# Second layer's modulation vectors: from the two second MLP products into the first layer's first MLP product and the second layer's mixers

## Chip, cores and metric

One core of a Trainium2 chip runs one inference step of a two-layer backbone. The metric is the device time of one execution in microseconds (us). Engines are named as in the profile: PE is TensorE (matmul), DVE is VectorE, ACT is ScalarE, POOL is GpSimd, SP issues the DMAs. A row of the profile names a line of the kernel (L286), the engine, the operation, and the tiles as "written<-read".

## The reference

Each of the two layers first turns a conditioning vector into six modulation vectors per conditioning row (there are two rows: the latent request and the context):

```python
m = silu(cond) @ w_mod + b_mod            # 6 * 1024 values per layer and row
sh1, sc1, g1, sh2, sc2, g2 = split(m, 6)
h  = rms_norm(x, norm1) * (1 + sc1) + sh1
mix = concat(A(h), B(h), C(h)) @ w_out    # RG-LRU, HGRN2, neighbourhood attention
x  = x + g1 * mix
h2 = rms_norm(x, norm2) * (1 + sc2) + sh2
x  = x + g2 * (square(relu(h2 @ w1)) @ w2)
```

x holds 1152 tokens (1024 latent, 128 context) of 1024 features; w1 is 1024 x 4096 and w2 is 4096 x 1024. The modulation of a layer is 48 tiles of 128 output features: tiles 0 to 7 are sh1, 8 to 15 sc1, 16 to 23 g1, 24 to 31 sh2, 32 to 39 sc2 and 40 to 47 g2. So tiles 0 to 15 are needed before a layer's first normalisation, 16 to 23 when its output projection is added to x, 24 to 39 before its MLP, and 40 to 47 only at the very end of the layer.

## The kernel before

Activations lie feature-major (128 features on the partitions, tokens along the free axis). Every large product is done in three passes over a high and a low part of each operand: ACT rounds the high part (`acopy`, L186), POOL or DVE subtracts it (`psub` L189, `vsub` L192). A layer has four stages, each written as a Python loop that a scheduler (`tc`) then orders for each engine by a simulated timeline and priorities; every engine runs its list in that order and waits where an operand is late.

1. Projections and mixers. `project` (tile `pj`) and `project_tokens` (tile `pt`) make the ten column groups; `rglru` (products `gr`, `gi`, line L740) runs beside the first of them and `hgrns` (products `sc`, L536, merged by the DVE at L541) beside the rest. `weave` alternates them in the source.
2. Attention (products `sl`, `tl`, `tc`, `av`) together with the output projection (tile `wo`), with the projections that are left over.
3. First MLP product (weights `ws`, L1110 to L1112): a one-level Strassen scheme, 16 column pairs times two token halves, 32 steps of 84 matmuls. The results are squared on ACT and DVE, combined and written to DRAM (`od`, `oraw`). Buffers `od_` (2) and `hx_` (3) are slices of one tile `spare`: in the first layer the tile that held silu(cond), named `sil`, in the second a tile `pad`.
4. Second MLP product (weights `wt`, operands `R`): 8 groups of operands come back from DRAM (`prepared_operands`), steps of 42 matmuls are accumulated in tiles `row` by the DVE (L198), the last group with the gate g2 (L210, `row<-z,mod,row`). Operands `R` take 18 slots in turn.

A modulation tile is made by `mod_tile` (L276): it loads 128 rows of the transposed w_mod into `wm` and lets the DVE multiply them by silu(cond) and sum along the row, once per conditioning row (L286, tile `junk` or `jk`); each such instruction is followed by a short one that reads its accumulator out. The tile is cut in as many pieces as the buffer is wide: with a ring of 384 columns (`g_`, or `sqt`, the four buffers of squares) three pieces, six instructions; with the ring `hr_` (1152 columns) one piece of 1024, two instructions.

Where the tiles are made, before: the first layer's 16 to 47 beside its own mixers, in small pieces (`mods`, 10 tiles beside `rglru`, 22 beside `hgrns`); the second layer's 0 to 39 in steps 2 to 44 of the first layer's second MLP product, in pieces of 1024 (`MODS2`); the second layer's 40 to 47 in the same steps of the second layer's second MLP product.

## Time and profile before

| | us |
|---|---|
| median of 3 runs | 3270.18 (3263.32 to 3278.54) |
| profiled execution | 3276.47 |
| its span, first to last instruction | 3274.7 |
| PE busy | 2960.4 (90% of the span) |
| DVE busy | 2406.1 (73%) |
| ACT busy | 1641.4 (50%) |
| POOL busy | 1567.8 (48%) |

The profiled execution lies 1.77 us above its own span and 6.3 us above the median of the runs. Busy times are shares of the whole span and mix stages with different limits; a window row gives, for one stretch, its length and then for PE, weight loads, DVE, ACT and POOL the busy time with the number of instructions in brackets, then the granted TensorE clock as a share of full speed, the busy share of the DMA engines and GB/s. The stages lie as follows: first layer's mixers to 537 us, attention and output projection to 833, first MLP product to 1235, second to 1678; second layer's mixers to 2117, attention and output projection to 2441, first MLP product to 2839, second to 3247.

### The profile page before, as it was taken

The page shows a single profiled execution, that of the slowest core. Times are in us where ns is not written, and L with a number is a line of the kernel's source. Part 1 is how long each engine was busy: PE and PEld are TensorE (multiplying, and loading weights), DVE is VectorE, ACT ScalarE, POOL GpSimd, SP SyncE. Part 2 cuts the span into 40 slices and gives each one's busy share as a digit, 9 for nine tenths or more (in the row PEclk, how much of TensorE's full clock was granted, in tenths as well). Part 3 has the DMA queues.
Part 4 walks back from the last instruction along what each step waited for, and adds up shares of the span by engine and source line. Part 5 has one row for each costly group of instructions (what it writes and reads, how often), then busy time and mean ns, then how long its engine had stood idle before and what let it go on. Part 6 is the DMA issues. An engine that isn't in the chain of part 4 may idle for free. (4 is left out here: it accounts for less than half of the span.)

```text
span 3274.7 us, 61327 instructions
## 1 busy us (share of the span) xinstructions
PE 2960.4 (90%) x21208; PEld 2815.3 (86%) x21208; DVE 2406.1 (73%) x5283; ACT 1641.4 (50%) x4079; POOL 1567.8 (48%) x1528
## 2 busy tenths in 40 slices
PE   7888998998889998988868999999987999899995
PEld 7878888798789998888858889988977999899994
DVE  8899974667885568998874677346779755777787
ACT  5543234565566666344454533345646566654443
POOL 4541132345676665554545311334556765654453
PEclk8989999999899998999979999999998999999997
DMA  7342447983455567675522102689634655855552
GB/s 270 91 108 87 132 121 224 283 269 103 158 176 185 177 212 279 216 245 198 181 94 74 58 29 80 183 239 293 220 127 148 194 179 181 281 204 173 185 194 68
DMA packets 391318, 566.48 MB, mean 173 GB/s; under 512 B 45920, under 2 KB 250848, under 8 KB 391008
## 3 DMA queue, kind: packets, MB, share of 16 engines
q1 hardware_dynamic: 391008, 562.57, 53.8%
q8 instruction: 167, 2.74, 0.4%
q14 instruction: 143, 1.17, 0.1%
HBM read 397.01 MB, written 165.42 MB: 172 GB/s over the span
## 5 line engine op out<-in xcount | busy, mean ns | idle before, releaser
L189 POOL TENSOR_TENSOR wl<-wr,wh 128x512 fp32r<-128x512 f32 x164 | 231.1, 1413 | 485.4 <-ACT wh L186 379.2
L189 POOL TENSOR_TENSOR wt<-wl,wt 128x256 fp32r<-128x256 f32 x276 | 258.0, 942 | 176.5 <-ACT wt L186 116.5
L1110 PE MATMUL bB<-R,wt 128*128 128x288 f32 x768 | 236.9, 309 | 63.7 <-ACT bB L186 40.8
L189 POOL TENSOR_TENSOR ws<-wl,ws 128x512 fp32r<-128x512 f32 x160 | 227.5, 1426 | 121.4 <-ACT ws L186 121.3
L421 PE MATMUL pj<-hh,wh 128*128 128x384 f32 x640 | 223.7, 354 | 27.0 <-ACT g L213 12.3
L1110 PE MATMUL bB<-t,ws 128*128 128x288 f32 x768 | 231.7, 302 | 18.0 <-DVE hr L198 9.6
L423 PE MATMUL pj<-hh,wl 128*128 128x384 f32 x640 | 225.1, 352 | 7.1 <-POOL wl L189 7.1
L1111 PE MATMUL bB<-R,wt 128*128 128x288 f32 x768 | 231.1, 301 | 0.0
L1112 PE MATMUL bB<-R,wt 128*128 128x288 f32 x768 | 230.0, 300 | 0.0
L1111 PE MATMUL bB<-t,ws 128*128 128x288 f32 x768 | 229.6, 299 | 0.0
L1112 PE MATMUL bB<-t,ws 128*128 128x288 f32 x768 | 229.2, 299 | 0.0
L422 PE MATMUL pj<-hh,wh 128*128 128x384 f32 x640 | 223.4, 350 | 0.0
L1110 PEld LDWEIGHTS bB<-R,wt 128*128 128x128 f32 x768 | 148.2, 193 | 74.2 <-ACT bB L186 48.3
L186 ACT CAST wt<-wl 128x256 fp32r<-128x256 f32 x288 | 115.9, 406 | 159.8 <-PE bB L1112 82.0
L421 PE MATMUL wo<-u,wh 128*128 128x288 f32 x512 | 160.1, 314 | 17.1 <-DVE x L210 13.4
L1110 PEld LDWEIGHTS bB<-t,ws 128*128 128x128 f32 x768 | 147.6, 192 | 22.0 <-DVE hr L198 11.4
L186 ACT CAST wh<-wr 128x512 fp32r<-128x512 f32 x164 | 101.1, 618 | 129.3 <-PE pj L422 65.2
L207 POOL TENSOR_SCALAR pl<-pl,rc 128x384 f32<-128x384 f32 x128 | 79.1, 618 | 176.5 <-DVE rc L952 83.9
L1110 PE MATMUL bA<-R,wt 128*128 128x288 f32 x512 | 156.0, 305 | 8.1 <-DVE row L210 5.8
L1112 PE MATMUL bA<-t,ws 128*128 128x288 f32 x512 | 155.4, 304 | 8.0 <-DVE ws L192 6.5
L1110 PE MATMUL bA<-t,ws 128*128 128x288 f32 x512 | 155.1, 303 | 4.3 <-ACT ws L186 2.3
L1111 PE MATMUL bA<-R,wt 128*128 128x288 f32 x512 | 154.6, 302 | 0.0
(363 smaller groups left out, 11364.9 us busy)
## 6 DMA issues: line engine op xcount, KB each, us to landing
wr<-in_w SPq DMA_DIRECT2D x304, 256.0 KB, 3.3
R<-od SPq DMA_DIRECT2D x96, 576.0 KB, 5.6
xb<-or SPq DMA_DIRECT2D x128, 288.0 KB, 4.2
wm<-in_w_mod SPq DMA_DIRECT2D x64, 512.0 KB, 5.6
od<-sil SPq DMA_DIRECT2D x96, 288.0 KB, 2.9
od<-pad SPq DMA_DIRECT2D x96, 288.0 KB, 3.1
wr<-in_w_in SPq DMA_DIRECT2D x104, 256.0 KB, 3.0
bi<-in_bias SPq DMA_DIRECT2D x96, 192.0 KB, 4.5
```

Of the source, the lines that this page charges most:

```text
L186: nc.scalar.copy(out=out, in_=in_)
L189: nc.gpsimd.tensor_tensor(out=out, in0=a, in1=b, op=ALU.subtract)
L207: nc.gpsimd.tensor_scalar(out=out, in0=a, scalar1=s1, scalar2=s2, op0=op0, op1=op1)
L421: mm(ps, lhsT=wh(k), rhs=ah(k), start=k == first, stop=False)
L422: mm(ps, lhsT=wh(k), rhs=al(k), start=False, stop=False)
L423: mm(ps, lhsT=wl(k), rhs=ah(k), start=False, stop=k == last)
L1110: mm(ps, lhsT=w[:, 0, ti(i)], rhs=t[:, 0], start=start and i == 0, stop=False, skip_group_check=True)
L1111: mm(ps, lhsT=w[:, 0, ti(i)], rhs=t[:, 1], start=False, stop=False, skip_group_check=True)
L1112: mm(ps, lhsT=w[:, 1, ti(i)], rhs=t[:, 0], start=False, stop=i == n - 1, skip_group_check=True)
```

## The change

- The second layer's tiles 0 to 15 are made in the first layer's first MLP product, from step 10 to step 30 of 32, through `sqt` (three pieces a tile). Since silu(cond) is needed there, it is loaded again at step 8 into the tile `sil`, which until then serves as `spare`; from then on the first layer's `od_` buffers come from `xr_` (two, as before) and `hx_` from `sqt`, the four buffers that the pieces of w_mod also use.
- Tiles 16 to 47 of the second layer are made beside its own mixers, by the same call and at the same places as in the first layer; `mods` no longer stops at the first layer. silu(cond) is kept until the second layer's mixers end, and no longer loaded in the second layer's MLP.
- Both second MLP products lose their modulation tiles, and with them the scratch tile `jk`.
- The 18 operand slots of the second MLP product are now three pools (4, 11 and 3) instead of two (7 and 11) with the turn started at the fourth slot. `gel` of the second layer comes from `g_` instead of a pool of its own, the gate weights `gw` from `xt`.

```diff
-MODS2 = (2, 44)
+MLP_MODS = (10, 30)
...
         def mods(n, piece):
             for j in take(left, n):
-                mod_tile(0, j, piece)
+                mod_tile(l, j, piece)
                 yield
 
-        left = iter(range(16, 48 if l == 0 else 16))
+        left = iter(range(16, 48))
...
+        later = iter(range(16))
         n = 0
         for v, (j, qs) in enumerate(first):
...
+                if not last and n == MLP_MODS[0] - 2:
+
+                    od_, hx_ = repeat(lambda: xr_("od")), repeat(lambda: sqt("hx")[:, :BLK])
+                    for c in range(2):
+                        load_cond(c)
+                if not last:
+                    for e in take(later, steps(16, MLP_MODS, n - 1)):
+                        mod_tile(l + 1, e, sqt)
         line.end()
...
-        tp0 = phase(st0, "tp0", 7, T, "right")
+        tp0, tp1 = phase(st0, "tp0", 4, T, "right"), phase(st0, "tp1", 3, T, "right")
...
-        junk1 = phase(st0, "jk", 1, DM // 2, "right")("jk").bitcast(mybir.dt.bfloat16)
-        tp1 = phase(st1, "tp1", 11, T, "right")
-
-        turn = cycle([tp0] * 7 + [tp1] * 11)
-        run_out(take(turn, 3))
+        tp2 = phase(st1, "tp2", 11, T, "right")
+
+        turn = cycle([tp0] * 4 + [tp2] * 11 + [tp1] * 3)
...
-        for c in range(2):
-            load_cond(c)
-        later = iter([(1, j) for j in (range(40, 48) if last else range(40))])
-        n_later, n = (8 if last else 40), 0
...
-                    n += 1
-                    for a in take(later, steps(n_later, MODS2, n)):
-                        mod_tile(*a, hr_, junk1)
```

What the engines are given can be read from the two programs' instruction lists. First the DVE in the first layer's first MLP product, one step before (`hr` and the slices of `sil` hold squared results, `wl` the sums of weights, `s` and `bB`, `bC` the product's accumulators):

```order
L198 TENSOR_TENSOR sil<-bC,s_12525 128x288
L210 SCALAR_TENSOR_TENSOR sil<-sil 128x288
L192 TENSOR_TENSOR hr<-sil,hr 128x288
L192 TENSOR_TENSOR sil<-hr,sil 128x288
L192 TENSOR_TENSOR wl<-wr 128x512
L192 TENSOR_TENSOR hr<-hr 128x288
L192 TENSOR_TENSOR sil<-sil,hr 128x288
L198 TENSOR_TENSOR hr<-bB,s_12656 128x288
L198 TENSOR_TENSOR sil<-bC,s_12656 128x288
L192 TENSOR_TENSOR wl<-wr,wl 128x512
```

and the same stretch of a step now, the slices of `sil` having become `hx`:

```order
L198 TENSOR_TENSOR hx<-bC,s_12151 128x288
L210 SCALAR_TENSOR_TENSOR hx<-hx 128x288
L192 TENSOR_TENSOR wl<-wr,wl 128x512
L192 TENSOR_TENSOR hr<-hx,hr 128x288
L192 TENSOR_TENSOR hx<-hr,hx 128x288
L192 TENSOR_TENSOR hr<-hr 128x288
L198 TENSOR_TENSOR wl<-wr 128x512
L286 ISA junk,ma<-wm,sil,par_106 128x384
L286 ISA ma 128x1
L192 TENSOR_TENSOR hx<-hx,hr 128x288
```

Between the step's own instructions stand the pieces of a modulation tile, each with its read of the accumulator; such a step has six pieces, 16 of the steps have them.

Next the DVE in the second layer's HGRN2, at the start of a block (`q`, `qb`, `kb`, `kf` are the decayed queries and keys, `ff` and `tot` the decays, `L` and `K` what the products `sc` read). Before:

```order
L198 TENSOR_TENSOR qb<-q,ff 128x384
L198 TENSOR_TENSOR q<-q,ff 128x384
L198 TENSOR_TENSOR qb<-qb,ff 128x192
L183 COPY L<-q 128x192
L183 COPY K<-kf 128x192
L198 TENSOR_TENSOR tot<-ff 128x192 x2
L198 TENSOR_TENSOR kb<-kb,ff 128x192
L198 TENSOR_TENSOR q<-q,ff 128x192
L198 TENSOR_TENSOR kf<-kf,ff 128x192
```

and now:

```order
L198 TENSOR_TENSOR qb<-q,ff 128x384
L286 ISA junk,mod_117<-wm,sil,ma 128x256
L286 ISA mod_117 128x1
L198 TENSOR_TENSOR q<-q,ff 128x384
L286 ISA junk,ma<-wm,sil,par_106 128x384
L286 ISA ma 128x1
L198 TENSOR_TENSOR qb<-qb,ff 128x192
L183 COPY L<-q 128x192
L183 COPY K<-kf 128x192
L198 TENSOR_TENSOR tot<-ff 128x192 x2
```

The same chain is now broken by pieces. From the first `xc` to the first merged `sc` there are 77 pieces among 124 other instructions, and from there to the last merged `sc` 115 among 461; the first layer has 77 among 123 and 115 among 462 there, before and now.

Last, PE at the third job of the second layer's attention (`tl` and `tc` transpose its softmax, `av` is its product with the values, `pj` are projections that are left over, `wo` is the output projection). Before, leftover projections stand between the transposes:

```order
L992 MATMUL av<-ptc,vc 64x128
L908 MATMUL sx<-ck,QS 128x256 x2
L992 MATMUL av<-ptc,vc 64x128 x3
L914 MATMUL sl<-KS,QS 128x384 x4
L967 MATMUL tl<-ident,pl 128x128 x3
L421 MATMUL pj<-hh_20201,wh 128x384
L422 MATMUL pj<-hh_20201,wh 128x384
L423 MATMUL pj<-hh_20201,wl 128x384
```

and now:

```order
L423 MATMUL pj<-hm_20376,wl 128x384
L421 MATMUL pj<-hm_20382,wh 128x384
L422 MATMUL pj<-hm_20382,wh 128x384
L423 MATMUL pj<-hm_20382,wl 128x384
L914 MATMUL sl<-KS,QS 128x384 x2
L967 MATMUL tl<-ident,pl 128x128 x6
L974 MATMUL tc<-ident,pc 128x128 x4
L421 MATMUL wo<-u,wh 128x288
L992 MATMUL av<-ptl,V 64x128 x6
L992 MATMUL av<-ptc,vc 64x128
```

In the new list the transposes of that job follow its scores with no projection between, and the output projection begins right behind them. The first layer's list has this order before and now: more of the projections stand beside HGRN2, and fewer are left for the attention.

## Rows read from the trace of the kernel before

**Rows 1.** The page: span, and part 1 (engine busy us, share, instructions).

```profile
span 3274.7 us, 61327 instructions
PE 2960.4 (90%) x21208; PEld 2815.3 (86%) x21208; DVE 2406.1 (73%) x5283; ACT 1641.4 (50%) x4079; POOL 1567.8 (48%) x1528
```

**Rows 2.** Windows, both second MLP products: stretch: length, busy (count) per engine, clock, DMA.

```profile
1247.20:1595.40 348.20, 317.43 (x2256) 310.61 (x2256) 316.73 (x612) 156.21 (x393) 179.57 (x164) 0.97 0.67 227
2851.20:3165.80 314.60, 306.07 (x2256) 303.53 (x2255) 230.61 (x467) 156.85 (x393) 152.37 (x164) 0.99 0.58 198
```

**Rows 3.** Tile row, first layer: count, ns min/median/max, first and last start, forms.

```profile
L186 ACT COPY row<-bA x8: 390/396/449, 1247.2 to 1287.8; 128x288 f32<-128x288 f32 x8
L210 DVE SCALAR_TENSOR_TENSOR row<-z,mod,row x32: 269/439/929, 1595.4 to 1671.6; 128x224 f32<-128x224 f32 x16, 128x64 f32<-128x64 f32 x16
```

**Rows 4.** Groups by form, DVE, line 286: count, busy us, mean ns.

```profile
L286 DVE CUSTOM_DVE_ANT_0 jk<-wm,sil,par 128x1024 bf16<-128x1024 f32 x96 | 136.7, 1424 | 7.8 <-ACT sil L213 4.4 <-DMA wm<-in_w_mod 3.3
L286 DVE CUSTOM_DVE_ANT_0 junk<-wm,sil,ma 128x384 bf16<-128x384 f32 x64 | 47.2, 738 | 3.6 <-DMA wm<-in_w_mod 2.8
L286 DVE CUSTOM_DVE_ANT_0 junk<-wm,sil,par 128x384 bf16<-128x384 f32 x64 | 44.7, 699 | 7.4 <-DMA wm<-in_w_mod 6.7
L286 DVE CUSTOM_DVE_ANT_0 junk<-wm,sil,ma 128x256 bf16<-128x256 f32 x64 | 38.8, 606 | 0.7
L286 DVE DVE_READ_ACCUMULATOR2_ANT mod<- 128x1 f32 x160 | 12.6, 78 | 0.0
L286 DVE DVE_READ_ACCUMULATOR2_ANT ma<- 128x1 f32 x128 | 10.3, 81 | 0.0
```

**Rows 5.** Tile wm, first layer's mixers.

```profile
L286 DVE CUSTOM_DVE_ANT_0 junk<-wm,sil,ma x128: 453/605/1669, 119.5 to 416.1; 128x384 bf16<-128x384 f32 x64, 128x256 bf16<-128x256 f32 x64
L286 DVE CUSTOM_DVE_ANT_0 junk<-wm,sil,par x64: 587/614/1694, 114.3 to 413.0; 128x384 bf16<-128x384 f32 x64
```

**Rows 6.** Waits of PE, both second MLP products: total us, times, longest.

```profile
PE bB L1110 <- ACT bB L186: 24.3, 17, 2.4
PE bB L1110 <- ACT bB L186: 6.6, 5, 2.2
```

**Rows 7.** Windows, first gr product to last wo product, both layers.

```profile
117.30:833.40 716.10, 650.32 (x4782) 592.89 (x4783) 549.21 (x1554) 317.90 (x845) 251.00 (x294) 0.95 0.54 159
1758.60:2440.70 682.10, 643.61 (x4784) 586.64 (x4783) 420.34 (x1159) 320.83 (x847) 246.85 (x294) 0.97 0.48 144
```

**Rows 8.** Windows, RG-LRU and HGRN2 stretches, both layers.

```profile
117.30:233.90 116.60, 91.40 (x491) 82.64 (x491) 103.65 (x222) 55.55 (x100) 53.76 (x46) 0.91 0.35 85
233.90:480.80 246.90, 231.24 (x1794) 211.66 (x1794) 231.62 (x731) 82.51 (x207) 55.20 (x57) 0.98 0.38 111
1758.60:1858.90 100.30, 85.19 (x464) 77.19 (x462) 49.99 (x83) 56.36 (x101) 50.25 (x46) 0.93 0.14 34
1858.90:2059.40 200.50, 195.79 (x1607) 178.09 (x1607) 155.84 (x474) 70.76 (x177) 36.19 (x39) 0.97 0.20 58
```

**Rows 9.** Waits of PE, first layer, RG-LRU to output projection.

```profile
PE pj L421 <- ACT g L213: 12.3, 1, 12.3
PE tc L974 <- ACT pc L213: 7.5, 1, 7.5
```

**Rows 10.** ACT in order of time, first attention: start us, us, group, idle before.

```profile
563.96 0.72 ACT L213 ACTIVATE ck<-ckr,sel 128x512 fp32r<-128x512 f32 x1 [8.92 <-DMA ckr<-in_cache_k]
```

**Rows 11.** Windows, second layer's projections with TensorE full.

```profile
1725.00:1750.00 25.00, 25.00 (x147) 25.00 (x146) 10.05 (x13) 9.66 (x18) 16.65 (x13) 1.00 0.40 131
```

**Rows 12.** Windows, first layer's first MLP product.

```profile
975.00:1175.00 200.00, 200.00 (x1510) 200.00 (x1509) 113.11 (x166) 121.63 (x281) 129.93 (x114) 1.00 0.57 184
1175.00:1200.00 25.00, 25.00 (x191) 25.00 (x190) 22.08 (x28) 15.74 (x36) 17.39 (x15) 1.00 0.53 169
```

**Rows 13.** Instruction groups by form, DVE, in the same stretch.

```profile
L192 DVE TENSOR_TENSOR hr<-sil,hr 128x288 f32<-128x288 f32 x21 | 20.0, 952 | 0.7
L192 DVE TENSOR_TENSOR hr<-hr 128x288 f32<-128x288 f32 x20 | 10.0, 501 | 1.1
```

More of the change, by code (lines that the diff above doesn't have):

```diff
@@ L1 @@
 from contextlib import ExitStack, nullcontext
-from itertools import cycle
+from itertools import cycle, repeat
 import concourse.bass as bass
@@ L274, in build, with mod_tile @@
     am = [C.tile([P, 16, 2], F32, name=f"am{l}") for l in range(DEPTH)]
-    def mod_tile(l, j, piece, junk=junk):
+    def mod_tile(l, j, piece):
         acc = [pcol(l, "bm", j)] * 2
@@ L1331, in e @@
             def e(n, ps):
-                gel[i][n] = (gl_ if l and n < 2 else xt)("gel")
+                gel[i][n] = (g_ if l and n < 2 else xt)("gel")
                 act(gel[i][n], ps, AF.Gelu_apprx_tanh)
@@ L1434, in build @@
                         run_out(project(win(m), ht, e, (n,)))
-        gw = [g_("gw")[:, :2 * P] for _ in range(4)]
+        gw = [(xt if l else g_)("gw")[:, :2 * P] for _ in range(4)]
         for j in range(4):
@@ L1536, in build @@
         if l:
-            gl_st.close()
+            sil_st.close()
         h_st, x4_st = ExitStack(), ExitStack()
@@ L1639, in build @@
         oraw = tc.dram_tile([NG, 2, len(SUMS), P, 2 * BLK], F32, name=f"or{l}")
-        od_ = cycle([spare[:, i * 2 * BLK:(i + 1) * 2 * BLK] for i in range(2)])
-        hx_ = cycle([spare[:, i * BLK:(i + 1) * BLK] for i in range(4, 7)])
+        od_ = cycle([lambda i=i: spare[:, i * 2 * BLK:(i + 1) * 2 * BLK] for i in range(2)])
+        hx_ = cycle([lambda i=i: spare[:, i * BLK:(i + 1) * BLK] for i in range(4, 7)])
         st = ExitStack()
@@ L1684, in part @@
             def part(p, t):
-                o = next(od_).bitcast(F32R).rearrange("p (j m) -> p j m", j=2)
+                o = next(od_)().bitcast(F32R).rearrange("p (j m) -> p j m", j=2)
                 acopy(o[:, 0], t)
@@ L1715, in c1 @@
             def c1(r, ps):
-                t = next(hx_) if r else ft("hr")[:, :BLK]
+                t = next(hx_)() if r else ft("hr")[:, :BLK]
                 act(t, ps, AF.Relu)
@@ L1721, in c2 @@
             def c2(r, ps):
-                t = ft("hr")[:, :BLK] if r else next(hx_)
+                t = ft("hr")[:, :BLK] if r else next(hx_)()
                 vtt(t, ps, on.s5, ALU.add)
@@ L1759, in build @@
             sil_st.close()
-        sil_st = ExitStack()
-        sil = phase(sil_st, "sil2", 1, 2 * DM)("sil").rearrange("p (c d) -> p c d", c=2)
+        if not last:
+            sil_st = ExitStack()
+            sil = phase(sil_st, "sil2", 1, 2 * DM)("sil").rearrange("p (c d) -> p c d", c=2)
+            for c in range(2):
+                load_cond(c)
         h_st, row_st, st0, st1 = (ExitStack() for _ in range(4))
@@ L1859, in build @@
                         st1.close()
-                        sil_st.close()
                         if not last:
-                            gl_st = ExitStack()
-                            gl_ = phase(gl_st, "gl", 4)
                             H = h_st.enter_context(tc.tile_pool(name="h", bufs=1, reuse_waits="tile"))
```

## The prediction

> **What bounds the kernel now.** I read the page first, then windows stage by stage. PE is busy for 90% of the span [rows 1], so a microsecond counts only where PE stands still or runs at half clock. The kernel holds its own comparison: each stage runs twice, once per layer, with the same matmuls and with different numbers of modulation tiles beside them.
>
> In the second MLP product, the stretch from the first copied block to the first gated add of the last group [rows 3] has 2256 matmuls in both layers. With 40 tiles (first layer) it lasts 348.2 us and DVE is busy for 316.7; with 8 tiles it lasts 314.6 with DVE at 230.6 [rows 2]. The waits say why: PE waits for ACT's copy into `bB`, which itself waits for the DVE's adds into `row`, 24.3 us in the first layer and 6.6 in the second [rows 6]. There the DVE is the bound.
>
> In the mixers, attention and output projection it is the other way round: the first layer has 32 tiles and needs 716.1 us, the second none and needs 682.1, for 4782 and 4784 matmuls [rows 7]. The excess lies in PE's idle time (65.8 against 38.5 us) and in a lower granted clock (0.95 against 0.97). In the first MLP product PE is full, at full clock, with DVE at 57% [rows 12].
>
> So the change takes tiles from a stage where they cost time, and puts two thirds of them where the first layer shows that they cost time too.
>
> **The change, part by part.** A tile in one piece is two instructions of 1.424 us and two reads of 0.078: 3.0 us of DVE. A tile in three pieces costs, from the first layer's 32, (47.2 + 44.7 + 38.8 + 10.3 + 64 x 0.078) / 32 = 4.56 us [rows 4]. The 48 moved tiles thus grow from 144 to 219 us of DVE work; by stage: -120, +73, +146, -24.
>
> (a) First layer's second MLP product loses 40 tiles. Thirty-two of them are worth 348.2 - 314.6 = 33.6 us, 1.05 us a tile. The last 8 can be worth at most what PE still idles beside them, 314.6 - 306.1 = 8.5 us [rows 2]; at least nothing. I take 4, the middle, since not all of the 6.6 us of waits [rows 6] stand near a tile. Together -37.6. The bounds: -42.1, and -17.7 if only the difference of the `bB` waits returns. What is late next is the operands `R`, as in the second layer, which the row of 314.6 contains.
>
> (b) Second layer's second MLP product loses the same 8: -4, between 0 and -8.5.
>
> (c) Second layer's mixers gain 32 tiles. The lists give them the first layer's places (77 pieces up to the first merged `sc`, 115 from there), and PE gets the first layer's order there, with few projections left for the attention. So the first layer is the measured price: 716.1 - 682.1 = +34.0 [rows 7]. It includes the three DMAs per tile that SP issues among the weights. One part of it is the first layer's own: a single 12.3 us wait of PE for ACT's `g` [rows 9]. There ACT has its three `mh` casts, which wait for the scan, ahead of both `g` evacuations; in the second layer's new list one `g` stands ahead of them, and PE gets 24 matmuls further, at 147 in 25 us [rows 11] about 4 us. So +30. The other long wait, 7.5 us of `tc` for ACT's `pc` [rows 9], comes from a load of cache_k that ACT waits for [rows 10]; before, leftover projections cover it in the second layer, and that cover goes with the new PE order. Bounds: the DVE idles for 50.3 us of the second layer's RG-LRU stretch and 44.7 of its HGRN2 stretch [rows 8]; 146 us of pieces less these 95 leaves +51. At the low end only the HGRN2 stretch pays, where PE idles for 15.7 us in the first layer and 4.7 in the second: +11. I stay near +34, because that row has the same tiles between the same instructions.
>
> (d) The first MLP product gains 16 tiles in 20 steps. A step of 84 matmuls lasts 200 x 84 / 1510 = 11.1 us, of which the DVE uses 6.3 [rows 12]; a tile of 4.56 us makes 10.9, and one step in five has none. Over 222 us that is 125.7 + 73 = 199 us of DVE. The row with 22.08 of 25 us shows PE still full at 88% DVE [rows 12]. What saturation costs is read from the second product: 230.6 - 24 + 120 = 327 us of DVE work took 348.2, a factor of 1.066 [rows 2]. 199 x 1.066 = 212, under 222: nothing. The upper bound has POOL in the way. POOL is busy for 65% here [rows 12] and for 22% in the first layer's HGRN2 stretch [rows 8]; the DVE's `hr<-sil,hr` lasts 0.952 us while `hr<-hr`, of the same shape and also with two inputs, lasts 0.501 [rows 13]. With 0.45 us on top of the shortest pieces (0.587 and 0.453 [rows 5]) a tile becomes 4 x 1.04 + 2 x 0.90 + 0.48 = 6.4 us, the stage 125.7 + 103 = 229, times 1.066 = 244: +22. The nearest row is the tile beside a POOL at 52% [rows 2], where a piece lasts 1.424 us, and that leads to the low end. I take +4, for the shared ring: `hx` and the pieces now take turns in four buffers, and in SP's queue the pieces' DMAs wait for a buffer ahead of weight loads, which are asked for seven operands, about one step, early.
>
> The Trainium skill ("SBUF — State Buffer", section "Who interferes with whom") says that a VectorE instruction with two SBUF inputs and a GpSimd instruction that reads SBUF exclude each other, each for the whole instruction. The pair of 0.952 and 0.501 us agrees with it. By the rule a piece that meets a POOL instruction waits for all that is left of it, which is the upper bound of (d); by the tile's row in the second product it waits for little.
>
> At nothing I cost the operand slots (4, 11, 3 taken from the first are the same succession as 7 and 11 taken from the fourth), the two loads and Silu activations of the conditioning (as many as before, beside an ACT that is busy for 61% in the first MLP product [rows 12]), and `gel` and `gw` in other rings; if one of them shows, it is a wait of a few us at the start of the second layer's RG-LRU.
>
> Sum: -37.6 - 4 + 30 + 4 = -7.6. The profiled execution took 3276.47 us, 1.8 more than its span, so 3268.9 for such a one; it lies 6.3 above the median of 3270.18, and from the median the sum gives 3262.6, rounded to 3263.
>
> **Rivals.** First, the second layer absorbs the tiles better than the first does: (c) is +11 and (d) 0. For it: the first layer's DVE idles for only 13 us of its RG-LRU stretch, the second's for 50 [rows 8], so there the ten tiles beside RG-LRU (57 us at most) nearly fit, and the long waits [rows 9] may be the first layer's own. Against it: the instruction lists are nearly the same, and in the HGRN2 stretch the DVE has 156 of 200 us taken already. Sum -37.6 - 4 + 11 = -30.6: 3240.
>
> Second, on the other side: POOL's lock makes the first MLP product DVE-bound. It decides from a tile of (222 / 1.066 - 125.7) / 16 = 5.2 us, 0.6 over the first layer's. At +22 there, with the mixers' full +34 and no gain from the 8 tiles (-33.6 only), the sum is +22.4: 3293. For it: POOL at 65% and the 0.952 us. Against: the second product's pieces of 1.424 us beside a POOL at 52%, and the ring of weights seven deep, which carries PE over single late steps.
>
> Third, that the tiles are not moved at all: the lists show that they are.
>
> **How the numbers follow.** A measurement of this kernel tells about 0.5% from no change, 16 us. The forecast, between 3254 and 3284 by itself, gets 0.50, the better absorption 0.31, the lock 0.19. The first holds "faster by over 0.5%" (under 3254), the last "slower" (over 3286), the forecast the middle. The range takes in both rivals' times, 3238 to 3292; what is left out is both ends at once: (c) at 51 with (d) at 22, or (a) at -42 with (c) under 11.
>
> **What would show it.** Right: in the first layer's second MLP product the stretch of 2256 matmuls lasts 308 to 312 us and its `bB` waits are under 8 us; the second layer's `gr` to `wo` lasts about 712 us with a DVE at 90% in HGRN2 and a wait of `tc` at the start of attention; the first MLP product keeps its length within 6 us, with pieces of about 0.7 us. Wrong: pieces over 1 us there and PE under 24 of 25 us with waits for DVE or ACT `hx`; or a `gr` to `wo` stretch under 698 us.

## The result, and the profile after

The changed kernel takes 3327.39 us (3325.78 to 3334.93, 4 runs), the kernel before beside it 3267.09 (3263.32 to 3278.54): a ratio of 1.0177, interval 1.0159 to 1.0195. It is slower by 60 us, where 3263 was forecast and 3292 was the top of the range. The profiled execution took 3326.2 us.

The page of the changed kernel, span and busy time, against [rows 1]:

```profile
span 3323.4 us, 61897 instructions
PE 2969.8 (89%) x21208; PEld 2826.0 (85%) x21208; DVE 2471.2 (74%) x5667; ACT 1635.2 (49%) x4079; POOL 1546.9 (47%) x1528
```

PE does the same matmuls; the span grows by 48.7 us in which it waits or runs at a lower clock. The windows of the changed kernel (columns as in [rows 2]), in this order: first layer's first MLP product (last `wo` to first product with `R`), its second MLP product, the second layer's `gr` to `wo`, the second layer's second MLP product, and the 200 us of [rows 12]:

```profile
826.70:1278.50 451.80, 387.02 (x2678) 378.72 (x2676) 358.27 (x595) 241.18 (x569) 272.30 (x217) 0.93 0.58 185
1305.40:1608.00 302.60, 299.85 (x2219) 299.04 (x2220) 202.13 (x428) 152.03 (x383) 144.75 (x160) 0.99 0.52 177
1775.10:2494.00 718.90, 650.98 (x4788) 593.67 (x4787) 548.06 (x1546) 320.21 (x847) 253.73 (x294) 0.95 0.54 159
2908.80:3213.80 305.00, 301.87 (x2258) 300.69 (x2257) 207.16 (x436) 154.84 (x392) 148.62 (x165) 1.00 0.54 182
975.00:1175.00 200.00, 182.90 (x1303) 180.79 (x1302) 154.48 (x274) 100.69 (x242) 121.56 (x100) 0.96 0.57 183
```

and the first product of the kernel before, the same stretch:

```profile
833.40:1234.80 401.40, 369.82 (x2676) 365.15 (x2675) 282.30 (x399) 245.97 (x576) 269.37 (x222) 0.96 0.57 183
```

Of the first product's 50.4 us, 33.2 are added idle time of PE (64.8 us against 31.6), and 17.2 are the same matmuls taking longer (387.0 against 369.8 us busy, at a granted clock of 0.93 against 0.96).

Cut at the same events, the span's 48.7 us come together like this (us; the last row is what lies between these stretches):

| stretch | before | after | difference | forecast |
|---|---|---|---|---|
| first MLP product, first layer | 401.4 | 451.8 | +50.4 | +4 (d) |
| from there to the first copied `row` | 12.4 | 26.9 | +14.5 | 0 |
| second MLP product, first layer | 348.2 | 302.6 | -45.6 | -37.6 (a) |
| `gr` to `wo`, second layer | 682.1 | 718.9 | +36.8 | +30 (c) |
| second MLP product, second layer | 314.6 | 305.0 | -9.6 | -4 (b) |
| all else | | | +2.2 | 0 |

Two of these rows must be read together, since the first copied `row` does not cut the same work: 2256 matmuls lie in the second MLP product's stretch before [rows 2] and 2219 after. From the first product with `R` to the first gated add it is the same work, before and after:

```profile
1234.80:1595.40 360.60, 326.68 (x2304) 319.17 (x2305) 329.12 (x629) 162.72 (x408) 188.10 (x171) 0.96 0.68 232
1278.50:1608.00 329.50, 315.56 (x2303) 313.90 (x2304) 220.98 (x456) 164.42 (x417) 160.07 (x176) 0.96 0.55 189
```

That is -31.1 us for both rows. The 37 matmuls that changed sides are worth about 5 us (305.0 us for 2258 in the second layer), so as an estimate the second product gained about 41 us and its start lost about 10.

So the two gains came and were somewhat larger than forecast, and the loss sits in the first MLP product, where 16 tiles cost 50 us. PE's waits there in the changed kernel:

```profile
PE bB L1110 <- DVE hr L198: 32.4, 17, 3.4
PE bB L1110 <- ACT bB L186: 9.6, 3, 6.1
```

and the first of these in the same stretch before:

```profile
PE bB L1110 <- DVE hr L198: 4.0, 2, 2.4
```

PE waits until the DVE has taken the sums of a hidden row out of the bank `bB`. What the DVE waits for, in the same stretch of the changed kernel:

```profile
DVE junk L286 <- DMA wm<-in_w_mod: 38.2, 15, 4.8
DVE ws L192 <- ACT ws L186: 13.8, 6, 7.4
DVE wl L192 <- POOL ws L189: 10.5, 8, 2.5
```

And its instructions, from 975 to 1175 us of the changed kernel, grouped by form (mean ns behind the busy time), against [rows 13]:

```profile
L192 DVE TENSOR_TENSOR hr<-hx,hr 128x288 f32<-128x288 f32 x16 | 19.2, 1202 | 0.4
L286 DVE CUSTOM_DVE_ANT_0 junk<-wm,sil,par 128x384 bf16<-128x384 f32 x22 | 16.6, 755 | 27.0 <-DMA wm<-in_w_mod 27.0
L286 DVE CUSTOM_DVE_ANT_0 junk<-wm,sil,ma 128x384 bf16<-128x384 f32 x22 | 14.4, 656 | 0.6
L192 DVE TENSOR_TENSOR hr<-hr 128x288 f32<-128x288 f32 x15 | 14.1, 939 | 0.8
L210 DVE SCALAR_TENSOR_TENSOR hx<-hx 128x288 f32<-128x288 f32 x16 | 13.7, 856 | 0.4
L286 DVE CUSTOM_DVE_ANT_0 junk<-wm,sil,ma 128x256 bf16<-128x256 f32 x22 | 10.6, 483 | 0.6
L198 DVE TENSOR_TENSOR hr<-bB,s 128x288 f32<-128x288 f32 x15 | 6.8, 453 | 1.6 <-PE bB L1112 1.6
```

Two causes offer themselves. The pieces wait for their loads, 27.0 us of 200, and everything behind them on the DVE waits too (late loads). Or the DVE has too much to do: `hr<-hx,hr` and `hr<-hr` grew from 952 and 501 ns to 1202 and 939, while `hr<-bB,s`, which reads one operand from PSUM, kept its 453 ns.

### The profile page after: what moved, and what is told of

Same layout as the page of the kernel before. It is cut to its first block, busy times and chain, and to the rows that moved or that the text cites. A ratio compares the mean times of both kernels' runs of the same rounds, so it can differ in the third digit from the quotient of the medians.

```text
span 3323.4 us, 61897 instructions
## 1 busy us (share of the span) xinstructions
PE 2969.8 (89%) x21208; PEld 2826.0 (85%) x21208; DVE 2471.2 (74%) x5667; ACT 1635.2 (49%) x4079; POOL 1546.9 (47%) x1528
## 5 line engine op out<-in xcount | busy, mean ns | idle before, releaser
L189 POOL TENSOR_TENSOR wt<-wl,wt 128x256 fp32r<-128x256 f32 x276 | 230.6, 839 | 189.2 <-ACT wt L186 123.2
L1110 PE MATMUL bB<-t,ws 128*128 128x288 f32 x768 | 237.4, 310 | 56.5 <-DVE hr L198 40.5
L1112 PE MATMUL bB<-t,ws 128*128 128x288 f32 x768 | 233.9, 305 | 0.0
L1111 PE MATMUL bB<-t,ws 128*128 128x288 f32 x768 | 233.8, 304 | 0.0
L286 DVE CUSTOM_DVE_ANT_0 junk<-wm,sil,ma 128x384 bf16<-128x384 f32 (+1 forms) x320 | 211.8, 662 | 6.9 <-DMA wm<-in_w_mod 2.1
L1110 PE MATMUL bA<-R,wt 128*128 128x288 f32 x512 | 156.0, 305 | 16.7 <-ACT row L186 6.6
```

Of the source, the lines that this page charges most:

```text
L189: nc.gpsimd.tensor_tensor(out=out, in0=a, in1=b, op=ALU.subtract)
L286: nc.vector.tensor_tensor_reduce(out=junk[:, :w], in0=r[:, :w], in1=sil[:, c, k0:k0 + w], scale=1.0, scalar=acc[c], op0=ALU.mult, op1=ALU. ...
L1110: mm(ps, lhsT=w[:, 0, ti(i)], rhs=t[:, 0], start=start and i == 0, stop=False, skip_group_check=True)
L1111: mm(ps, lhsT=w[:, 0, ti(i)], rhs=t[:, 1], start=False, stop=False, skip_group_check=True)
L1112: mm(ps, lhsT=w[:, 1, ti(i)], rhs=t[:, 0], start=False, stop=i == n - 1, skip_group_check=True)
```

## Experiments

All ratios are against the kernel before on the same chip. "First product" is the stretch from the last `wo` to the first product with `R` in the first layer (401.4 us before, 451.8 after); "start" is the stretch behind it (12.4 and 26.9).

| run | first product | start | ratio (95%) |
|---|---|---|---|
| no_tiles | 406.1 | 24.0 | 1.0015 (0.9999 to 1.0031) |
| no_loads | 443.4 | 24.2 | 1.0135 (1.0111 to 1.0158) |
| own_ring | 444.1 | 20.7 | 1.0122 (1.0098 to 1.0146) |
| tiles_in_mlp2 | 400.0 | 15.2 | 1.0043 (1.0026 to 1.0060) |
| paced_no_loads | 439.3 | 24.9 | 1.0148 (1.0127 to 1.0169) |
| paced_own_ring | 444.0 | 21.2 | 1.0111 (1.0086 to 1.0136) |
| paced_own_cond | 434.6 | 15.3 | 1.0099 (1.0083 to 1.0116) |
| no_mixer_tiles | 450.0 | 26.9 | 1.0026 (1.0014 to 1.0038) |
| psum_ops | 411.7 | 24.5 | 1.0037 (1.0020 to 1.0054) |
| sbuf_ops | 453.5 | 24.9 | 1.0166 (1.0137 to 1.0194) |
| paced_long | 428.5 | 18.7 | 1.0075 (1.0053 to 1.0096) |
| paced_half | 411.2 | 25.3 | 1.0040 (1.0022 to 1.0058) |
| psum_after | 407.8 | 21.9 | 1.0013 (1.0000 to 1.0026) |
| sbuf_after | 446.2 | 25.3 | 1.0134 (1.0119 to 1.0149) |
| mixers_16 | 398.7 | 15.6 | 1.0045 (1.0029 to 1.0061) |
| mixers_8 | 395.4 | 15.6 | 1.0018 (1.0006 to 1.0030) |

Each run has one profile. Four of them have no tile in this stretch and the hidden rows where they were (the kernel before, tiles_in_mlp2, mixers_16, mixers_8); their first product lasts 395.4 to 401.4 us, so a difference of 5 us there is not clear of what one profile differs from the next. The diffs show the main lines of each edit; vectors that a run then leaves out are constants.

**First: which part of the change costs the 50 us.**

```diff
 # no_tiles
-        later = iter(range(16))
+        later = iter(())
 # no_loads, in mod_tile
-            r = piece("wm")
+            r = piece("wm") if load else sil[:, 1, k0:min(k0 + NW, DM)]
 # own_ring (one buffer fewer for w1 makes the room)
-W1_RING, W2_RING = (7, 7), 11
+W1_RING, W2_RING = (6, 7), 11
+        wm_ = phase(st, "wm", 3, NW, "right")
-                        mod_tile(l + 1, e, sqt)
+                        mod_tile(l + 1, e, wm_)
 # tiles_in_mlp2: nothing in the first product, later = range(16) in the second
+                    for e in take(later, steps(16, (2, 44), n)):
+                        mod_tile(l + 1, e, hr_, junk1)
```

> Leaves out the second layer's first 16 modulation tiles (their vectors stay zero); the reload of silu(cond) and the new places of the prepared hidden rows stay. In the changed kernel the first layer's first MLP product, from the last output projection to the first product of the second MLP, takes 451.8 us against 401.4 before, and 26.9 us more pass until the second product copies out (12.4 before). Late loads: the pieces of w_mod come late and everything behind them on VectorE with them, so without them the stretch is 401 to 408 and the kernel 3275 to 3285. Work on VectorE: the same here. Moved buffers: the new places of od and hx and the reload cost the 50 us, so the stretch stays 440 to 452 and the kernel 3315 to 3327. The start of the second product stays at 27 if od's place alone makes it late, falls to 12 if the pieces do.

> The 16 tiles of the first MLP product are formed from data that already lie in SBUF (silu(cond) itself), so their 96 reductions stay on VectorE with their lengths and no w_mod is loaded; those 16 tiles' values are another thing than the reference's. Late loads: the stretch falls to 402 to 415, the kernel to 3275 to 3292. Work on VectorE: it stays at 440 to 452, the kernel at 3315 to 3327. Moved buffers: the same 440 to 452.

> The pieces of w_mod in the first MLP product get three buffers of their own instead of the ring of four that they share with the hidden rows; the ring of w1 has 6 buffers instead of 7 to make room. Late loads, by way of the shared ring (a piece waits until a hidden row has been stored): the stretch falls to 405 to 425, the kernel to 3280 to 3300. Late loads, by way of SyncE's queue (a load stands behind stores that wait for their data): it stays at 440 to 452, the kernel at 3315 to 3327. Work on VectorE: 440 to 452. Moved buffers: some of it goes if hx in the shared ring is what costs, 430 to 450.

> Undoes one part of the change: the first 16 tiles are formed in the first layer's second MLP product again, in whole halves of 1024 columns, with the hidden rows' places as before; the other 32 stay in the second layer's mixers. Every theory on the first product gives it back its 401 us and the start its 12; 16 tiles of 24 x 96/40 reductions lie beside 348.2 us before and 302.6 without any, so this stretch is 303 if VectorE hides them all and 321 if the cost goes by the number. Kernel 3327.4 - 50.4 - 14.5 + (0 to 18) = 3262 to 3281; 3262 to 3268 is what I take, since VectorE has room. If the 50 us came of something else (a clock that stays low), it is 3300 or more.

Without tiles the first product is back at 406.1: the moved buffers and the reload of silu(cond) cost some 5 us there, not 50. Without loads it stays at 443.4, so the reductions alone cost 37 us, and the loads some 8. Pieces in buffers of their own give 444.1, the same 8 us, and the whole kernel 3320.46: the shared ring was a small part. The theory of late loads as the main cause, which had 402 to 415 for no_loads, fell here. tiles_in_mlp2 gave the first product back its 400 us, but the kernel took 3293.3 us, 12 over the top of its forecast; the kernel before was also 12 slower on that chip (3279.2), and as a ratio, 1.0043, it is that top. The second product took 320.3 us; with its start it took 335.5 us, against 321.5 in paced_own_cond (below), which has no tiles there and `od` in the same place, so 16 tiles cost about 0.9 us each.

One thing was not held in no_loads and own_ring: the scheduler, no longer held back by loads, drew the tiles together. In the trace mostly 11 or 12 reductions stand between two rows' sums, against 2 to 7 in the changed kernel.

**Second: one tile in a step at most, the start, and the mixers.** A tile's first reduction now takes its bias through a number that ACT makes from the hidden row of the step, which ties it there (6 reductions between two rows' sums, in 16 of the 32 steps).

```diff
 # paced_*, in c2 of a step that has a tile
+                    act(p, t[:, :1], AF.Identity, scale=0.0, bias=pcol(l + 1, "bm", e))
 # paced_own_cond besides: od_ and hx_ stay in spare; 5 buffers for w1 instead of 7
-                    od_, hx_ = repeat(lambda: xr_("od")), repeat(lambda: sqt("hx")[:, :BLK])
+            sil = phase(st, "silm", 1, 2 * DM, "right")("sil").rearrange("p (c d) -> p c d", c=2)
 # no_mixer_tiles
-        left = iter(range(16, 48))
+        left = iter(range(16, 48 if l == 0 else 16))
```

> As no_loads (reductions over data that already lie in SBUF, so the 16 tiles have other values), but each tile's first reduction needs a number taken from the hidden row of its own step, so that at most one tile, 6 reductions, stands between two rows' sums on VectorE (12 in no_loads, 3 to 7 in the changed kernel). First product 443.4 us in no_loads, 406.1 without tiles. Crowding (VectorE hides one tile in a step of 12.3 us and not two): 406 to 413, kernel 3285 to 3296. Work as such (every reduction costs its place): 430 to 445, kernel 3310 to 3327. Late loads alone as the cause in the changed kernel: 406 to 413 too.

> As own_ring (the pieces of w_mod in three buffers of their own, six buffers for w1), with the same pacing: one tile at most between two rows' sums, and its loads may run ahead of it. First product 444.1 us in own_ring. Crowding: 406 to 415, kernel 3280 to 3295; if loads late behind SyncE's stores cost as well, 420 to 435, kernel 3295 to 3310. Work as such: 435 to 450, kernel 3315 to 3327.

> The hidden rows' od and hx keep the places that they have before; silu(cond) of the first MLP product lies in 8 kB of its own (the ring of w1 has 5 buffers instead of 7 for it), the pieces of w_mod have the ring of four alone, and the tiles are paced. If od's place on the right side makes the start of the second product late, its 26.9 us fall to 12 to 16 here (24.0 without tiles showed that the tiles are not the reason). Crowding: first product 400 to 412; kernel 3327 - 45 - 11 = 3265 to 3285. Work as such: 430 to 445, kernel 3300 to 3315. A ring of w1 that is now too short would show as TensorE waiting for ws.

> The changed kernel without the 32 tiles of the second layer's mixers (those modulation vectors stay zero). The mixers take 718.9 us in the changed kernel's profile, 724 to 729 in three others with the same tiles, 682.1 before. If the tiles alone make the difference: 680 to 685, kernel 3280 to 3290. If the place of gw and the GELU's rows, or silu(cond) kept longer, has a share: 690 to 710, kernel 3290 to 3310.

Crowding by itself fell: paced, without a single load, the first product still takes 439.3. paced_own_cond, with loads in a ring of their own and the hidden rows in their old places, takes 434.6, 33 over the kernel before. Its shorter ring for `w1` shows a little: PE waits 6.9 us in 2 times for the DVE's `ws`, 2.1 before.

The start has a mechanism in the changed kernel's trace: the first copy of `row` waits for a store of `od` (waits from 1278.5 to 1310 us; PE waits behind that copy):

```profile
PE bA L1110 <- ACT row L186: 6.6, 1, 6.6
...
ACT row L186 <- DMA od<-od: 4.7, 1, 4.7
```

This wait is about 5 us of ACT and 6.6 of PE. In paced_own_cond, where `od` stayed, it is gone, and the start takes 15.3 us, as in tiles_in_mlp2; in the runs that moved `od` the start takes 18.7 to 26.9, tiles or none. But 83 or 84 matmuls stand in the start of these, 43 to 50 in the others, so part of that is work that changed sides. And own_ring, paced_own_ring and paced_long moved `od` too, with 6 buffers for `w1`, and their first copy waits for no store. From the first product with `R` to the first gated add these three take 320 to 322 us, paced_own_cond 321.5, and the changed kernel, for the same matmuls, 329.5; no_tiles, with the wait, 325.8. So the wait costs 4 to 8 us, and moving `od` alone does not bring it. That `row` lies over the buffers of `od` where it comes, and not in those three, is likely and not shown.

no_mixer_tiles brings the second layer's `gr` to `wo` stretch back to 679.1 us: the 32 tiles alone make its difference, and `gel`, `gw` and the longer life of silu(cond) cost nothing that shows. (Fourteen profiles with these 32 tiles, the changed kernel's among them, have 718.9 to 729.2 us there, with 723 in the middle, so its own 718.9 is the lowest. The first layer's stretch, with the same 32 tiles and no change in it, has 708 to 717 in all profiles.)

What one step looks like in paced_no_loads, in order of time (start us, duration us), first the DVE:

```profile
1101.51 1.56 DVE L287 CUSTOM_DVE_ANT_0 junk<-sil,pace 128x384 bf16<-128x384 f32 x1 [1.69 <-ACT pace L213]
1103.00 0.08 DVE L287 DVE_READ_ACCUMULATOR2_ANT ma<- 128x1 f32 x1
1103.00 0.45 DVE L198 TENSOR_TENSOR hx<-bC,s 128x288 f32<-128x288 f32 x1
1103.37 0.60 DVE L287 CUSTOM_DVE_ANT_0 junk<-sil,pace 128x384 bf16<-128x384 f32 x1
1103.90 0.08 DVE L287 DVE_READ_ACCUMULATOR2_ANT ma<- 128x1 f32 x1
1103.90 1.34 DVE L192 TENSOR_TENSOR wl<-wr,wl 128x512 f32<-128x512 f32 x1
1105.17 1.55 DVE L210 SCALAR_TENSOR_TENSOR hx<-hx 128x288 f32<-128x288 f32 x1
```

and POOL in the same time:

```profile
1101.36 1.30 POOL L189 TENSOR_TENSOR ws<-wl,ws 128x512 fp32r<-128x512 f32 x1 [3.77 <-ACT ws L186]
1103.88 0.81 POOL L189 TENSOR_TENSOR od<-hr,od 128x288 fp32r<-128x288 f32 x1 [1.23 <-ACT od L186]
1104.70 1.69 POOL L189 TENSOR_TENSOR ws<-wl,ws 128x512 fp32r<-128x512 f32 x1
```

Two reductions of one form take 1.56 and 0.60 us. The long one starts 0.15 us after a POOL instruction and ends 0.41 us after that has ended (1101.51 + 1.56 against 1101.36 + 1.30); the short one begins while POOL stands. `wl<-wr,wl` and `hx<-hx` end 0.55 and 0.33 us after the POOL instruction that was under way when they began. So it looks as if these DVE instructions wait for POOL's to end and then run; the next round puts that to the test.

**Third: turns with POOL, or any work on the DVE.** Instead of tiles, 8 plain products per step that nobody uses, with one operand from PSUM or from SBUF; and tiles in fewer instructions, or fewer tiles.

```diff
 # psum_ops; sbuf_ops with sil[:, 1, i * 64:i * 64 + BLK] in place of ps
+                    for i in range(8):
+                        vtt(junk[:, :BLK], ps, on.s5, ALU.mult)
 # against paced_no_loads. paced_long: two reductions of 1024 columns a tile
 # (6 buffers for w1, a longer junk); paced_half: 8 tiles
-            r = piece("wm") if load else sil[:, 1, k0:min(k0 + NW, DM)]
+            r = piece("wm") if load else sil[:, 1]
-                es = list(take(later, steps(16, MLP_MODS, u))) if r and not last else []
+                es = list(take(later, steps(8, MLP_MODS, u))) if r and not last else []
```

> The changed kernel without the 16 tiles of the first MLP product (those vectors stay zero; 406.1 us in no_tiles), and in their 16 steps 8 plain products of 128x288 each on VectorE that nothing uses: one operand the bank bC in PSUM, the other the sums' row in SBUF, as in the evacuation hr<-bB,s that takes 0.45 us in every run. They add 8 x 0.45 = 3.6 us of VectorE to a step of 12.3. Turns with GpSimd (a VectorE instruction whose operands both lie in SBUF waits until GpSimd's instruction of the moment has ended, one from PSUM does not): each takes 0.45 and the stretch is 406 to 415. Work as such: 430 to 445, as with the tiles.

> The same 8 products in the same 16 steps, with the first operand in SBUF (silu(cond)) instead of PSUM. Turns with GpSimd: many of them last 0.9 to 1.6 us instead of 0.45, 6 to 9 us of VectorE in a step, and the stretch is 440 to 475. Work as such: as psum_ops, within 5 us.

> As paced_no_loads (439.3 us), each tile in 2 reductions of 1024 columns instead of 6 of 384, 384 and 256 (the ring of w1 has 6 buffers, for the longer output that nobody reads). Turns with GpSimd, by number of instructions: a third of the cost of 33 us above no_tiles stays, 412 to 422. Work by the columns: 2 x 1.42 us of VectorE instead of 3.75 to 6.0, so three quarters stay, 428 to 434.

> As paced_no_loads with 8 tiles instead of 16, at most one in two steps (the other 8 tiles' vectors stay zero). If VectorE, thrown back by one tile, catches up in the free step behind it: 406 to 412. If each tile costs its 2.1 us wherever it stands: 423.

411.7 against 453.5: nearly all of the cost hangs on where an operand lies. But in sbuf_ops the products had also been scheduled ahead of `hx<-bC,s`, where they waited 32.3 us for ACT's `s` (975 to 1200 us), so the fourth round has one order for both. paced_half shows that the cost is not linear: 8 tiles with a free step between them cost 5.1 us over no_tiles, 16 in nearly every step 33.2. paced_long missed the count of instructions (412 to 422) and came out where the columns put it: its reductions took 1.61 us each, and the waits for POOL fell on the other instructions (`hr<-hr` 1.20 us on average, `hx<-hx` 1.24, from 975 to 1200 us). So fewer instructions help, by 11 us, but by less than their number would.

**Fourth: the same order, and how the mixers' price grows.**

```diff
 # psum_after; sbuf_after with sil[:, 1, i * 64:i * 64 + BLK] in place of ps
+                        vtt(junk[:, :BLK], ps, t, ALU.mult)
 # mixers_16 (mixers_8 with 40): tiles 0 to 31 in the second product
+        later, n = iter(range(0 if last else 32)), 0
-        left = iter(range(16, 48))
+        left = iter(range(16 if l == 0 else 32, 48))
```

> As psum_ops, with the 8 unused products of a step forming the bank bC (PSUM) times the hidden row hx just written, so that they stand behind its evacuation and ahead of its square, in the same places of VectorE's order as in sbuf_after. Turns with GpSimd: 0.45 us each, first product 410 to 422 (a burst of 3.6 us ahead of hx's square instead of products spread out). Work or order as such: 430 to 455, equal to sbuf_after.

> As psum_after with silu(cond) from SBUF as the first operand and nothing else changed, order included. Turns with GpSimd: 0.7 to 0.9 us each, first product 430 to 460, and at least 15 us over psum_after. Order as such (sbuf_ops was long because its products waited for ScalarE's row): within 5 us of psum_after.

> Tiles 0 to 31 in the first layer's second MLP product, 32 to 47 in the second layer's mixers, none in a first MLP product. By the number: mixers 682 + 16 x 1.33 = 703, second product 302.6 + 32 x 1.13 = 339; kernel about 3293.3 - 21 + 18 = 3290 on the chip of tiles_in_mlp2. If VectorE in the mixers hides the first tiles as the first MLP product does when they stand apart (paced_half): mixers 685 to 692, kernel 3272 to 3280, as the kernel before.

> Tiles 0 to 39 in the first layer's second MLP product as in the kernel before, 40 to 47 in the second layer's mixers instead of its second MLP product. By the number: mixers 682 + 8 x 1.33 = 693, against 9.6 us saved in the second layer's second product: even with the kernel before, ratio 0.998 to 1.004. If the mixers hide the first tiles: 682 to 685, ratio 0.995 to 0.999, a little faster than the kernel before.

407.8 (a little under its forecast) against 446.2 us, with the same added instructions in the same places and one operand different. The added products as a group of the DVE, 975 to 1175 us of psum_after:

```profile
L198 DVE TENSOR_TENSOR junk<-bC,hx 128x288 bf16<-128x288 f32 x96 | 43.7, 455 | 2.6
```

and of sbuf_after:

```profile
L198 DVE TENSOR_TENSOR junk<-sil,hx 128x288 bf16<-128x288 f32 x85 | 77.2, 908 | 2.3
```

The window of the same 200 us, psum_after:

```profile
975.00:1175.00 200.00, 197.12 (x1472) 197.12 (x1473) 161.62 (x263) 123.01 (x286) 129.84 (x113) 0.98 0.57 184
```

and sbuf_after:

```profile
975.00:1175.00 200.00, 184.33 (x1315) 182.21 (x1316) 167.02 (x227) 106.67 (x255) 125.92 (x104) 0.95 0.49 158
```

From PSUM a product takes 455 ns and PE loses 2.9 us of 200; from SBUF it takes 908 ns on average and PE loses 15.7. The mean hides two kinds. In order psum_after and sbuf_after (count, shortest, median and longest in ns):

```profile
L198 DVE TENSOR_TENSOR junk<-bC,hx x96: 444/457/460, 1014.0 to 1165.7; 128x288 bf16<-128x288 f32 x96
L198 DVE TENSOR_TENSOR junk<-sil,hx x85: 444/951/1578, 1012.6 to 1173.7; 128x288 bf16<-128x288 f32 x85
```

In sbuf_after 50 of the 85 products start while a POOL instruction is under way: they last 0.94 to 1.58 us, and each ends 0.31 or 0.32 us after that POOL instruction. The 35 others last 0.44 to 0.46 us. In psum_after 65 of the 96 start beside a POOL instruction, and they last 0.44 to 0.46 us like the rest. So the wait for POOL's instruction of the moment is the cause, and an operand in PSUM avoids it.

The DVE is busy for 162 and 167 us, hardly different, but it does 263 instructions in the one and 227 in the other: in sbuf_after 85 x (908 - 455) ns = 38.5 us of the busy time are added products that stand and wait for POOL.

In the mixers the price per tile grows: 0 tiles 679.1 us, 8 tiles 685.4, 16 tiles 698.9, 32 tiles 718.9 to 729.2. The first 8 cost 0.8 us each, the last 16 between 1.2 and 1.9; the profiles with equal tiles differ by 10 us, and that of mixers_8 is its fastest execution, 11 us under the median, so that the price grows is likely and not shown. Neither distribution beats the kernel before: mixers_8 is slower by 0.06 to 0.3%, mixers_16 by 0.3 to 0.6%. mixers_16 met its time (3291 against 3290), but not by its parts: the second MLP product took 353.1 us where 339 was forecast. mixers_8, with the 40 tiles of the kernel before, takes 370.0 us there with the start, against 360.6; why is open. Its ratio is what its forecast by the number had (0.998 to 1.004). No other division was run; reductions whose silu(cond) lies in PSUM were not tried, since the kernel's eight buffers in PSUM are in use in that stage.

## Why the prediction was wrong, step by step

The step that failed is (d), "I take +4" with bounds of 0 and +22; it was +50.4. The runs divide it: some 4.7 us for the reload and the moved buffers (no_tiles; near what one profile differs from the next), which I had costed at nothing; 33 to 37 for the reductions as such (paced_no_loads, no_loads), which the sum had at nothing because the DVE seemed to have room; the rest, 8 to 12, goes when the loads go, or mostly when the pieces have buffers of their own (own_ring: 7.7). Of the last I had named the place ("the shared ring") and given it 4 us. Of the signs, "pieces over 1 us" did not come and "PE under 24 of 25 us" with waits for the DVE did: 182.9 of 200. Three reasons were wrong in the middle term:

- The price of a tile. I had both ends, 4.56 and 6.4 us, and went to the low one because the nearest row by POOL's share was the piece of 1.424 us, which I read as waiting for little. Its mean hides the waits:

```profile
L286 DVE CUSTOM_DVE_ANT_0 jk<-wm,sil,par x96: 1267/1278/2524, 1263.1 to 3069.7; 128x1024 bf16<-128x1024 f32 x96
```

  Of the first layer's 80, 35 start beside a POOL instruction and last 1.63 us on average, the 45 others 1.27. Nor is it near: it has 1024 columns, and it waits once, as a short one does. Such reductions in paced_long end 1.08 us (median) after the POOL instruction that they met, those of 384 columns in paced_no_loads 0.41 us; so three short ones can wait three times. Paced, a tile measured (28.7 + 21.0 + 16.1) / 11 + 6 x 0.08 = 6.5 us (22 reductions of each size from 975 to 1175 us), my upper end:

```profile
L287 DVE CUSTOM_DVE_ANT_0 junk<-sil,ma 128x384 bf16<-128x384 f32 x22 | 28.7, 1303 | 0.0
L287 DVE CUSTOM_DVE_ANT_0 junk<-sil,pace 128x384 bf16<-128x384 f32 x22 | 21.0, 953 | 11.9 <-ACT pace L213 11.9
L287 DVE CUSTOM_DVE_ANT_0 junk<-sil,ma 128x256 bf16<-128x256 f32 x22 | 16.1, 734 | 0.0
```

  The pair of 0.952 and 0.501 us in [rows 13] said so; I had read it and weighed it too low. In the changed kernel itself the pieces stayed short, (16.6 + 14.4 + 10.6) / 11 + 0.48 = 4.3 us a tile, my lower end, and the kernel's own instructions took the waits: that they would keep their 125.7 us was wrong.
- The capacity. I let the DVE be filled to 1/1.066, 94% of the stretch, by a factor from the second product. (The factor takes 327 us of DVE work from a sum; the row itself has 316.7 [rows 2], which gives 1.10 and 219 us, still under 222.) Here PE starves with the DVE busy for 154 of 200 us (77%) in the changed kernel and 83% in paced_no_loads, while in psum_after it is nearly full beside a DVE at 81%. The busy share counts waits for POOL as work, so it is no measure of room. The idle time can be split by what ended it. In the kernel before, from 975 to 1200 us, the DVE idles for 225 - 113.1 - 22.1 = 89.8 us [rows 12]; 28.7 + 16.3 = 45.0 of them are waits for PE and 40.5 waits of its list for POOL:

```profile
DVE sil L198 <- PE bC L1112: 28.7, 18, 2.7
DVE sil L192 <- POOL sil L189: 25.3, 15, 2.5
DVE hr L198 <- PE bB L1112: 16.3, 18, 1.2
DVE wl L192 <- POOL ws L189: 15.2, 11, 1.6
```

  One could take the waits for PE alone as room. psum_after speaks against it: its products added 43.7 us of work to 200 us, and PE lost 2.9 us of them, 4.2 in no_tiles. The DVE's longest waits from 975 to 1175 us in no_tiles:

```profile
DVE hx L198 <- PE bC L1114: 23.7, 16, 2.7
DVE hx L192 <- POOL od L189: 22.5, 13, 2.5
DVE wl L192 <- POOL ws L189: 18.8, 11, 4.1
DVE hr L198 <- PE bB L1114: 12.3, 14, 1.2
```

  and in psum_after:

```profile
DVE wl L192 <- POOL ws L189: 13.2, 13, 2.5
DVE hx L198 <- PE bC L1114: 12.0, 10, 2.7
DVE hx L192 <- POOL od L189: 3.8, 3, 2.4
```

  The added products went into both kinds of idle time. What did not fit was work that itself stands and waits for POOL. Why paced_half nearly hides its 8 tiles, by the free step behind each, is argued and not shown.
- "The row with 22.08 of 25 us shows PE still full at 88% DVE" [rows 12]. One slice of 25 us shows that PE can coast on rows already taken, not that the DVE has that much to give over 200 us.

The second rival named the right mechanism and its price of 22 us for it was too small (33 to 37 measured); I gave it 0.19, because of the 1.424 us row.

The Trainium skill ("SBUF — State Buffer", section "Who interferes with whom") has it as a rule that a VectorE instruction with two SBUF inputs contends with a GpSimd instruction that reads SBUF, and that one with at most one SBUF input does not. psum_after and sbuf_after bear it out (455 and 908 ns); I had set the reading of one row above it.

(a) was right in its mechanism and nearly in its size: over the same matmuls about -41 (estimated above) against -37.6, inside its bound of -42.1. The last 8 tiles were worth about 7 us, most of PE's idle time of 8.5 us beside them [rows 2], where I took the middle; the second layer's own stretch, which lost just 8, gave 9.6 (b, bound 8.5), and the clock of that stretch rose from 0.99 to 1.00.

(c) was right in mechanism and too small by 7 to 11: +36.8 in the changed kernel's profile and 41 by the middle of all profiles, inside the bound of +51. "So the first layer is the measured price" held for the DVE (548.06 us against 549.21 [rows 7]) and for the clock (0.95), and the stretch came out at 718.9 against 716.1; over all profiles it is 719 to 729 against 708 to 717, so the price was not quite the same. The -4 for a wait that was the first layer's own was given back by others: `sc` now waits for the DVE's `k` once, for 10.1 us.

The start of the second product, about 10 us without the matmuls that changed sides, was in no term: "the operand slots" and "`gel` and `gw` in other rings" were weighed as edits of buffers, and `od_` in `xr_` was not, though the first copy of `row` now waits for its store.

Forecast and measured sums: -37.6 - 4 + 30 + 4 = -7.6 against -45.6 - 9.6 + 36.8 + 50.4 + 14.5 + 2.2 = +48.7.

What stays open: how the 8 to 12 us of the loads divide between the ring and SP's queue, why the mixers cost more than the first layer's 34, and what of the start hangs on the places of the buffers.

## What to carry to other kernels

Before work is put on an engine that looks half idle, ask what that work itself will wait for there: neither the busy share nor the idle time by its ends told how much would fit, and 43.7 us of products that waited for nothing fitted where 77.2 us of them, 50 of 85 waiting for POOL, did not. On the DVE beside a busy POOL, price an added instruction by where its operands lie and by how many instructions there are, not by their columns alone, and look at the shortest and the longest of a group behind its mean. When a stretch is cut at two events, count its matmuls before and after. And when a buffer is moved, ask who last reads it and what takes its place next.

## What the runs showed of the hardware

The same product of 128x288 took 455 ns with one operand in PSUM and 908 ns on average with both in SBUF, beside a POOL busy for 63 to 65% of the time. All of the 50 that met a POOL instruction at their start in sbuf_after ended 0.31 to 0.32 us after it, so most or all of their work came behind it. It is not a matter of one kind of instruction: the reductions, the subtractions and the square `hx<-hx`, which reads one tile twice (480 ns on average in no_tiles, 856 in the changed kernel, from 975 to 1175 us), all take part. And the busy share counts it as work: 81 and 84% of 200 us for the DVE in a run where PE is nearly full and in one where it starves.
